# The Fourier branch computed on folded tokens: 129 of 256 output positions, the rest mirrored

## The chip, the cores and the metric

One core of one Trainium2 chip runs the whole program. The metric is the device time of one execution in microseconds (us), lower is better. The kernel before takes 1244.37 us (median of 3 runs, 1244.19 to 1245.08).

The engines are called by the profile's names: PE is TensorE's matrix multiply, PEld its weight loads, DVE is VectorE, ACT is ScalarE, POOL is GpSimd and SP is SyncE, which issues nearly all transfers. Each engine works through its own instructions in order and waits on the others by semaphores.

## The reference, cut to what matters

Two layers run over 256 latent tokens and 256 context tokens with 1024 channels. Every layer normalises and modulates the tokens, projects them with one combined weight (`h @ w_in`), feeds slices of the projection to four branches (retention, short convolution, Fourier mixing, pooling), merges the branches through sigmoid gates and one output projection, and ends with a SwiGLU feed-forward part. The last layer needs only the latent stream after the retention state of the context is known. The branch that changes is this one:

```python
def fourier_mix(u):                        # u: (1, 256 tokens, 256 channels)
    b, n, _ = u.shape
    z = jnp.fft.fft2(u.astype(jnp.float32).reshape(b, n, FFT_GROUPS, FFT_GROUP_DIM), axes=(1, 3), norm='ortho')
    return jnp.real(z).reshape(b, n, MIX).astype(u.dtype)
```

It is a two-dimensional Fourier transform, over 256 tokens and over 64 channels inside each of four groups, of which the real part is kept: with C and S the cosine and sine sums, the result is Cn(Cd u) - Sn(Sd u).

## The kernel before, in words

The kernel is one long list of `Step`s written out in order. A step names the weight blocks it needs, and a loop at the end of the program takes the steps one after the other: it first calls `Weights.pump`, then the step's own function, then (for a step with `tick`) one round of `tick`.

- `Weights` (L54 to L153) streams the weights. A block is 128 partitions by 1024 or 1280 values. It is loaded by SP (L94), cut into a rounded high part by ACT (L102, `hi`) and a low part by DVE (L112, `lo = raw - hi`). Blocks are cut up to two ahead of the step that is being written (`ahead=2`), in a ring of four.
- A projection `proj` (L660) of one block of 128 output channels takes 8 chunks of the contraction with three matmuls each (`mm3`, L205: hi*hi, lo*hi, hi*lo, all in the reduced fp32 type, one pass each). In layer 0 it streams 512 columns (256 latent and 256 context tokens, NS = 2), in layer 1 it streams 256 (NS = 1).
- Small side work, such as the Fourier branch after its projection, is put in a list `sides` of generators. After each ticking step, `tick` (L213) advances the first two of the list to their next `yield` and puts them at the end. The side work therefore sits in every engine's instruction order between the projections of the following steps.
- `bank` (L174) gives out PSUM banks in rotation: four of kind "a", three of kind "b". `ot` (L628) gives out SBUF tiles from a rotating pool of 5 (layer 0) or 4 (layer 1), which the convolution and pooling branches share; `sm` is a pool of small tiles, among them four "hf" tiles that `modulate` (L451) uses.

In layer 0 the order is: the opening with q, k and v, two gate projections (which start the retention side work `both`), then for each half c of the 256 branch channels the Fourier step and three convolution steps (`conv_cg`, `conv_xv`, `conv_bg`), then two pooling steps, then the big gate steps, which read the branch results `br`. In layer 1 the six convolution steps come first, while the context stream's last norms of layer 0's feed-forward part (`Chain`, L483: `one`, `two`, `three`, then four times `turn`, which transposes on PE and modulates on ACT and DVE) still run as side work. Then come the two Fourier steps, two gate steps, `drain_sides`, which writes out all side work that is left, and the value projection `v_step` (L688, tile `vps`).

In the Fourier branch (`fourier`, L853) the projection lands in PSUM with channels on partitions and tokens along the columns. ACT copies it to SBUF (`u`, L857). `rest` is the side work. Its first stage (L866, tile `fa`) transforms the channels: for each stream and each half of 128 tokens, one plain fp32 matmul with 128 tokens as the stationary operand and the 256 columns of `fcs` (cosine beside sine) as the moving one; ACT copies the result to `pf` (L868). Its second stage (L874, tile `fb`) transforms the tokens: per stream four accumulating fp32 matmuls, each with 128 stationary columns of `pf` and 256 moving columns of `fcn`. The result is cut into `br[2]` by `split` (ACT L202, DVE L203). A plain fp32 matmul shows as two PE instructions in the trace, with a weight load before each.

Of the kernel before, what the change touches and what calls it, by code (L numbers as in the profile page):

```python
# [8 lines left out]
F32 = mybir.dt.float32  # L9
F32R = mybir.dt.float32r  # L10
BF16 = mybir.dt.bfloat16
AF = mybir.ActivationFunctionType
ALU = mybir.AluOpType
# [4 lines left out]
P = 128  # L18
D = 1024
KC = D // P  # L20
SEQ = 256
# [8 lines left out]
LOG2E = 1.4426950408889634  # L30
VROW = 528
PIECE = 33
MOD_ORDER = (0, 2, 1, 3)
Q, K, V, G, BG, CG, XV, FU, PU, GATE = 0, 2, 4, 6, 8, 10, 12, 14, 16, 18
KEEP = 4
# [121 lines left out]
def kernel(ctx: ExitStack, tc: tile.TileContext, a: dict, out: bass.AP):  # L157
    ctx.enter_context(tc.manual_schedule())
    nc = tc.nc

    def pool(name, bufs=1, stack=ctx, **kw):
        return stack.enter_context(tc.tile_pool(name=name, bufs=bufs, reuse_waits="tile", **kw))
# [3 lines left out]
    sm = pool("sm", 4)  # L166
# [7 lines left out]
    def bank(tag, name, shape=None, keep=False):  # L174

        i = banks[tag].pop(0)
        if not keep:
            banks[tag].append(i)
        t = psum.tile([P, 512], F32, tag=f"bank{i}", name=name)
        return t if shape is None else cut(t, shape)  # L180
# [4 lines left out]
    def cut(t, shape):  # L185
        n = 1
        for x in shape:
            n *= x
        t = t[:, :n]
        if len(shape) == 2:  # L190
            t = t.rearrange("p (a b) -> p a b", b=shape[1])
        if len(shape) == 3:
            t = t.rearrange("p (a b c) -> p a b c", b=shape[1], c=shape[2])
        return t

    def load(pl, shape, src, name, eng=None, **kw):
        t = pl.tile(shape, F32, name=name, **kw)
        (eng or nc.sync).dma_start(t, src)
        return t

    def split(hi, lo, src):
        nc.scalar.activation(hi, src, AF.Copy)  # L202
        nc.vector.tensor_tensor(lo, src, hi.bitcast(F32), op=ALU.subtract)  # L203

    def mm3(ps, st, mv, first, last):  # L205

        nc.tensor.matmul(ps, lhsT=st[0], rhs=mv[0], start=first, stop=False)  # L207
        nc.tensor.matmul(ps, lhsT=st[0], rhs=mv[1], start=False, stop=False)  # L208
        nc.tensor.matmul(ps, lhsT=st[1], rhs=mv[0], start=False, stop=last)  # L209
# [21 lines left out]
    nc.vector.memset(mhalf, -0.5)  # L231
    two = dec.tile([P, 2 * PIECE], F32, name="two")
    nc.vector.memset(two, 2.0)
# [11 lines left out]
    bsel = load(cst, [P, 2], a["c_bsel"], "bsel", nc.scalar)  # L245
    e12 = load(dec, [P, 2, 2 * PIECE], a["c_e12"], "e12", nc.scalar)
    kexp = load(dec, [P, 2, 2], a["c_kexp"], "kexp", nc.scalar)
# [126 lines left out]
    def decays():  # L374
# [21 lines left out]
        yield  # L396
        y = dec.tile([P, 2 * PIECE], F32, name="dy")
        nc.vector.tensor_scalar(y, e12[:, 0, :], lg[:, 0:1], None, op0=ALU.mult)
        nc.vector.scalar_tensor_tensor(y, e12[:, 1, :], lg[:, 1:2], y, op0=ALU.mult, op1=ALU.add)
        ky = dec.tile([P, DEPTH, 2, 2, HEADS], F32, name="dky")  # L400
        for l in range(DEPTH):
            for jt in range(2):
                for d in range(2):
# [3 lines left out]
                    )  # L407
        v = dec.tile([P, 2 * PIECE], F32, name="dv")
        kf = ky.rearrange("p a b c d -> p (a b c d)")
# [4 lines left out]
        for i in range(2):  # L414
            nc.sync.dma_start(
                vscr[i].rearrange("a (b c) -> (a b) c", c=PIECE), v[:, i * PIECE : (i + 1) * PIECE]
            )
# [195 lines left out]
    def mixer(l, h, hnext, start=None):  # L613
        T = 512 if l == 0 else 256
        NS = T // SEQ
# [6 lines left out]
        def rt(tag, shape, name, bufs=1):  # L622
            n = 1
            for x in shape:
                n *= x
            return cut(P_["t"].tile([P, n], F32, tag=tag, name=name, bufs=bufs), shape)

        def ot(shape, name):  # L628
            return cut(P_["o"].tile([P, T + 32], F32, tag="o", name=name), shape)

        br, fix = [], {}
# [17 lines left out]
        def fixed():  # L649
            t = P_["t"]  # L650
            fix["rope"] = load(t, [P, 2, SEQ], a["c_rope"], f"rope{l}")
            fix["fcs"] = load(t, [P, 2 * P], a["c_fd"], f"fcs{l}")
            fix["fcn"] = load(t, [P, 2, 2, SEQ], a["c_fn"], f"fcn{l}")
            fix["inv"] = load(t, [P, 2, SEQ], a["c_inv"], f"inv{l}")
            for c in range(2):
                for j in range(2):
                    b = slice(j * DH, (j + 1) * DH)
                    nc.sync.dma_start(fix["pw"][b, c, b], a["pool_w"][l, 2 * c + j])

        def proj(blk, name, ps=None, cols=slice(0, T)):  # L660
            if ps is None:
                ps = bank(ptag[0], name)[:, :T]
            for k in range(KC):
                sl = slice(k * P, (k + 1) * P)
                mm3(
                    ps[:, cols],
                    (blk.hi[:, sl], blk.lo[:, sl]),
                    (h[0][k][:, cols], h[1][k][:, cols]),
                    k == 0,
                    k == KC - 1,  # L670
                )
            return ps
# [179 lines left out]

        def fourier(blk, c):  # L853

            ps = proj(blk, f"fu{l}{c}")
            u = ot([T], "fu")
            nc.scalar.activation(u, ps, AF.Copy)  # L857

            def rest():
                yield  # L860
                pf = []
                for s in range(NS):
                    pa = bank("a", f"fa{l}{c}{s}", [2, 2 * P])
                    for t in range(2):
                        lo = s * SEQ + t * P
                        nc.tensor.matmul(pa[:, t, :], lhsT=u[:, lo : lo + P], rhs=fix["fcs"], start=True, stop=True)  # L866
                    pf.append(ot([2, 2 * P], "pf") if NS == 2 else rt("pf", [2, 2 * P], "pf"))
                    nc.scalar.activation(pf[s], pa, AF.Copy)  # L868
                yield
                for s in range(NS):  # L870
                    pb = bank("a", f"fb{l}{c}{s}")[:, :SEQ]
                    for n in range(4):
                        t, j = n // 2, n % 2
                        nc.tensor.matmul(  # L874
                            pb,
                            lhsT=pf[s][:, t, j * P : (j + 1) * P],
                            rhs=fix["fcn"][:, t, j, :],
                            start=(n == 0),
                            stop=(n == 3),
                        )  # L880
                    sl = slice(s * SEQ, (s + 1) * SEQ)
                    split(br[2][0][c][:, sl], br[2][1][c][:, sl], pb)

            sides.append(rest())

# [150 lines left out]
        if l == 0:  # L1036
# [43 lines left out]
            for c in range(2):  # L1080
                add(fourier, FU + c, c)
                conv_steps(c)
# [358 lines left out]
    start = next(i for i, st in enumerate(mix0) if st.tick)  # L1441
# [34 lines left out]
def _layouts(v):  # L1476
# [4 lines left out]
    d["c_in"] = c(np.stack([v["c"][0].reshape(KC, P).T, v["c_ctx"].reshape(KC, P).T], 1))  # L1481
    wm = v["w_mod"][0].reshape(KC, P, 12, 512)[:, :, list(MOD_ORDER)]
    d["w_mod"] = c(wm.reshape(KC, P, 2, 2, 512).transpose(0, 2, 1, 3, 4)).reshape(KC, 2, P, 1024)
# [29 lines left out]
def _constants():  # L1513
    import numpy as np

    f4 = np.float32
    d = {"c_ident": np.eye(P, dtype=f4)}
    p = np.arange(P)
    d["c_bsel"] = ((p[:, None] // DH == np.arange(2)) / DH).astype(f4)
    e = (p[:, None] % 16) * PIECE + np.arange(PIECE) - 256  # L1520
    e = np.concatenate([e, -e], 1)
    d["c_e12"] = np.stack([np.maximum(e, 0), np.maximum(-e, 0)], 1).astype(f4)
    j = p[:, None] + P * np.arange(2)
    d["c_kexp"] = np.stack([255 - j, j], 2).astype(f4)
    freqs = (f4(10000.0) ** (-np.arange(16, dtype=f4) / f4(16))).astype(f4)
    n = np.arange(SEQ)
    pos = np.stack([n // 64, n % 64]).astype(f4)
    ang = pos[(p // 32) % 2] * freqs[p % 16][:, None]
    cos, sin = np.cos(ang).astype(f4), np.sin(ang).astype(f4)
    sin = np.where((p % 32 < 16)[:, None], -sin, sin)  # L1530
    d["c_rope"] = np.stack([cos, sin], 1).astype(f4)
    k = np.arange(DH)
    ph = 2 * np.pi * ((k[:, None] * k) % DH) / DH
    fd = np.zeros((P, 2, P))
    for g in range(2):
        s = slice(g * DH, (g + 1) * DH)
        fd[s, 0, s], fd[s, 1, s] = np.cos(ph), np.sin(ph)
    d["c_fd"] = fd.reshape(P, 2 * P).astype(f4)
    ph = 2 * np.pi * ((n[:, None] * n) % SEQ) / SEQ
    fn = np.stack([np.cos(ph), -np.sin(ph)], 1) / 128.0  # L1540
    d["c_fn"] = np.ascontiguousarray(fn.reshape(2, P, 2, SEQ).transpose(1, 0, 2, 3)).astype(f4)
    inv = np.zeros((P, 2, SEQ))
    for g, w in enumerate((2, 4, 8, 16)):
        cnt = np.clip(n - w // 2 + w, 0, SEQ) - np.clip(n - w // 2, 0, SEQ)
        inv[(g % 2) * DH : (g % 2 + 1) * DH, g // 2] = 1.0 / cnt
    d["c_inv"] = inv.astype(f4)
    return d
# [18 lines left out]
```

## Time and profile before

| | us |
|---|---|
| median of three runs | 1244.37 |
| the profiled execution | 1246.01 |
| its span, first to last instruction | 1244.2 |
| PE busy | 1205.8 |
| PEld busy | 1032.6 |
| DVE busy | 776.5 |
| ACT busy | 452.4 |

The span is what the profile draws; the 1.8 us between it and the execution's own time lie before and after the recorded instructions. Matmuls are pipelined, so the recorded lengths of neighbouring matmuls overlap: what one of them costs in a row of many is the distance from one start to the next, not its recorded length. The mean granted TensorE clock of the execution is 0.994 of full speed (2.4 GHz).

### The profile page before, as it was taken

The page shows a single profiled execution, that of the slowest core. Times are in us where ns is not written, and L with a number is a line of the kernel's source. Part 1 is how long each engine was busy: PE and PEld are TensorE (multiplying, and loading weights), DVE is VectorE, ACT ScalarE, POOL GpSimd, SP SyncE. Part 2 cuts the span into 40 slices and gives each one's busy share as a digit, 9 for nine tenths or more (in the row PEclk, how much of TensorE's full clock was granted, in tenths as well). Part 3 has the DMA queues.
Part 4 walks back from the last instruction along what each step waited for, and adds up shares of the span by engine and source line. Part 5 has one row for each costly group of instructions (what it writes and reads, how often), then busy time and mean ns, then how long its engine had stood idle before and what let it go on. Part 6 is the DMA issues. An engine that isn't in the chain of part 4 may idle for free.

```text
span 1244.2 us, 17237 instructions
## 1 busy us (share of the span) xinstructions
PE 1205.8 (97%) x6790; PEld 1032.6 (83%) x6790; DVE 776.5 (62%) x1242; ACT 452.4 (36%) x712; POOL 41.2 (3%) x39
## 2 busy tenths in 40 slices
PE   6999999999999989999999999989999999999997
PEld 2687878888888788888888888779889998999986
DVE  4454464477887465776777674475666666666644
ACT  3332332323322453222222222354335445444532
POOL 1500000000000000000000000000000000000000
PEclk9999999999999989999999999999999999999999
DMA  8542323546755224666756783343455563656662
GB/s 291 180 130 84 102 85 107 209 151 168 203 176 190 82 94 126 225 209 158 246 185 205 226 270 105 112 134 136 123 153 183 178 225 116 201 176 185 196 220 88
DMA packets 66433, 206.29 MB, mean 166 GB/s; under 512 B 14640, under 2 KB 18224, under 8 KB 66352
## 3 DMA queue, kind: packets, MB, share of 16 engines
q1 hardware_dynamic: 65200, 204.96, 52.8%
q8 instruction: 53, 0.87, 0.3%
q10 hardware_dynamic: 1152, 0.24, 0.1%
q14 instruction: 28, 0.23, 0.1%
HBM read 204.06 MB, written 1.11 MB: 165 GB/s over the span
## 4 chain that ended last, share of the span: by engine, by line
PE 89%; DVE 4%; ACT 3%; issue 1%; DMA 1%; POOL 0%; SPq 0%; DVEq 0%; POOLq 0%; ACTq 0%
PE up L208 10%; PE up L209 10%; PE up L207 10%; PE gate L207 7%; PE gate L209 7%; PE gate L208 7%; PE dn L209 4%; PE dn L208 4%; PE dn L207 4%; PE pb L209 2%; PE pb L207 2%; PE pb L208 2%; PE wo L209 1%; PE wo L207 1%; PE wo L208 1%
## 5 line engine op out<-in xcount | busy, mean ns | idle before, releaser
L317 DVE SCALAR_TENSOR_TENSOR mjunk<-raw_mod,crow 128x1024 bf16<-128x1024 f32 x128 | 156.4, 1222 | 11.1 <-DMA raw_mod<-in_w_modt 8.9
L208 PE MATMUL up<-hm0lo,hi_up 128*128 128x512 f32 (+1 forms) x384 | 143.6, 374 | 0.5 <-DVE hm0lo L449 0.5
L207 PE MATMUL up<-hm0hi,hi_up 128*128 128x512 f32 (+1 forms) x384 | 143.8, 375 | 0.0
L209 PE MATMUL up<-hm0hi,lo_up 128*128 128x512 f32 (+1 forms) x384 | 143.7, 374 | 0.0
L112 DVE TENSOR_TENSOR lo_up<-raw_up,hi_up 128x1024 fp32r<-128x1024 f32 x88 | 107.5, 1223 | 36.2 <-ACT hi_up L102 36.2
L112 DVE TENSOR_TENSOR lo_gt<-raw_gt,hi_gt 128x1280 fp32r<-128x1280 f32 x64 | 95.3, 1489 | 30.5 <-ACT hi_gt L102 30.2
L207 PE MATMUL gate<-h0hi,hi_gt 128*128 128x512 f32 x256 | 100.5, 392 | 0.0
L207 PE MATMUL up<-hm1hi,hi_up 128*128 128x256 f32 x352 | 100.3, 285 | 0.0
L208 PE MATMUL up<-hm1lo,hi_up 128*128 128x256 f32 x352 | 100.3, 285 | 0.0
L209 PE MATMUL up<-hm1hi,lo_up 128*128 128x256 f32 x352 | 100.1, 284 | 0.0
L209 PE MATMUL gate<-h0hi,lo_gt 128*128 128x512 f32 x256 | 99.6, 389 | 0.0
L208 PE MATMUL gate<-h0lo,hi_gt 128*128 128x512 f32 x256 | 99.6, 389 | 0.0
L102 ACT ACTIVATE hi_up<-raw_up 128x1024 fp32r<-128x1024 f32 x88 | 92.1, 1048 | 7.2 <-DMA raw_up<-in_w_up 6.6
L102 ACT ACTIVATE hi_gt<-raw_gt 128x1280 fp32r<-128x1280 f32 x64 | 81.0, 1266 | 28.0 <-DMA raw_gt<-in_w_gate 28.0
L112 DVE TENSOR_TENSOR lo_dn<-raw_dn,hi_dn 128x1024 fp32r<-128x1024 f32 x44 | 53.6, 1224 | 51.4 <-ACT hi_dn L102 51.2
L988 ACT ACTIVATE sg<-gate 128x512 f32<-128x512 f32 (+1 forms) x64 | 31.3, 490 | 148.1 <-PE gate L209 146.8
L208 PEld LDWEIGHTS up<-hm0lo,hi_up 128*128 128x128 f32 x384 | 73.4, 191 | 13.1 <-DVE hm0lo L449 0.7
L207 PEld LDWEIGHTS up<-hm0hi,hi_up 128*128 128x128 f32 x384 | 73.5, 191 | 12.6
L209 PEld LDWEIGHTS up<-hm0hi,lo_up 128*128 128x128 f32 x384 | 73.3, 191 | 12.4
L102 ACT ACTIVATE hi_dn<-raw_dn 128x1024 fp32r<-128x1024 f32 x44 | 46.4, 1058 | 91.8 <-PE dn L209 67.1
L207 PE MATMUL gate<-hf0hi,hi_gt 128*128 128x256 f32 x256 | 73.4, 287 | 0.0
L209 PE MATMUL gate<-hf0hi,lo_gt 128*128 128x256 f32 x256 | 72.4, 283 | 0.0
(327 smaller groups left out, 2759.7 us busy)
## 6 DMA issues: line engine op xcount, KB each, us to landing
raw_up<-in_w_up SPq DMA_DIRECT2D x88, 512.0 KB, 3.9
raw_gt<-in_w_gate SPq DMA_DIRECT2D x64, 640.0 KB, 4.0
raw_mod<-in_w_modt SPq DMA_DIRECT2D x80, 512.0 KB, 4.1
raw_dn<-in_w_down SPq DMA_DIRECT2D x44, 512.0 KB, 4.3
raw_in<-in_w_in SPq DMA_DIRECT2D x28, 512.0 KB, 3.7
raw_mod<-in_w_mod SPq DMA_DIRECT2D x16, 512.0 KB, 4.5
raw_wo<-in_w_o SPq DMA_DIRECT2D x16, 512.0 KB, 4.2
grow<-gscr SPq DMA_DIRECT2D x6, 512.0 KB, 7.4
```

The lines of the kernel that those rows point to most:

```text
L102: self.nc.scalar.activation(b.hi, b.raw, AF.Copy)
L112: self.nc.vector.tensor_tensor(b.lo, b.raw, b.hi.bitcast(F32), op=ALU.subtract)
L207: nc.tensor.matmul(ps, lhsT=st[0], rhs=mv[0], start=first, stop=False)
L208: nc.tensor.matmul(ps, lhsT=st[0], rhs=mv[1], start=False, stop=False)
L209: nc.tensor.matmul(ps, lhsT=st[1], rhs=mv[0], start=False, stop=last)
L317: nc.vector.scalar_tensor_tensor(junk, b.raw, 1.0, crow[s], op0=ALU.mult, op1=ALU.mult, accum_out=out()[:, s, i : i + 1])
L988: nc.scalar.activation(sg, ps, AF.Sigmoid)
```

## The change

With 256 tokens, cos and sin of token n and of token 256-n are equal and opposite, so the sums need only the folded tokens u[n] + u[256-n] (with cosines) and u[n] - u[256-n] (with sines), 128 of each; token 128 stands alone, and its part of output k is (-1)^k times its channel cosine sum. Output 256-k differs from output k only by the sign of the sine part, so 129 outputs are computed and 127 are mirrored.

- `u` gets a zero column behind the 256 tokens of each stream (a DVE memset). Behind the ACT copy, two DVE operations make the folded tiles (`fold`, the second operand read backwards), and a small copy keeps token 128 (`mid`). They stand in the Fourier step itself, not in the side work.
- The first stage has two matmuls per stream, each with 128 moving columns, in place of two with 256. The results of both streams share one bank and one ACT copy.
- The second stage has two matmuls per stream with 129 moving columns, not accumulated, in place of four with 256; and per half c one more with NS columns, the channel cosine sum of `mid`.
- Then, per stream: ACT copies the sine part (and the `mid` column) to SBUF (`si`, from the pool of "hf" tiles), DVE adds the alternating `mid` part to the cosine part, subtracts the sine part into the mirrored columns, and adds it into the plain ones. `split` now stands behind one more `yield`, once for both streams, and reads SBUF.
- `fcn` is 128 x 3 x 129 values in place of 128 x 2 x 2 x 256.

```diff
-            fix["fcn"] = load(t, [P, 2, 2, SEQ], a["c_fn"], f"fcn{l}")
+            fix["fcn"] = load(t, [P, 3, NK], a["c_fn"], f"fcn{l}")
...
             ps = proj(blk, f"fu{l}{c}")
-            u = ot([T], "fu")
-            nc.scalar.activation(u, ps, AF.Copy)
+            u = ot([NS, SEQ + 8], "fu")
+            nc.vector.memset(u[:, :, SEQ : SEQ + 1], 0.0)
+            nc.scalar.activation(u[:, :, :SEQ], ps.rearrange("p (s n) -> p s n", n=SEQ), AF.Copy)
+            eo = ot([2 * T // 2 + NS], "eo")
+            fold = [eo[:, j * NS * P : (j + 1) * NS * P].rearrange("p (s n) -> p s n", n=P) for j in range(2)]
+            mid = eo[:, 2 * NS * P : 2 * NS * P + NS]
+            for j, op in ((0, ALU.add), (1, ALU.subtract)):
+                nc.vector.tensor_tensor(fold[j], u[:, :, :P], u[:, :, P + 1 : SEQ + 1][:, :, ::-1], op=op)
+            nc.vector.tensor_copy(mid, u[:, :, P])
 
             def rest():
                 yield
-                pf = []
+                pa = bank("a", f"fa{l}{c}", [NS, 2, P])
                 for s in range(NS):
-                    pa = bank("a", f"fa{l}{c}{s}", [2, 2 * P])
-                    for t in range(2):
-                        lo = s * SEQ + t * P
-                        nc.tensor.matmul(pa[:, t, :], lhsT=u[:, lo : lo + P], rhs=fix["fcs"], start=True, stop=True)
-                    pf.append(ot([2, 2 * P], "pf") if NS == 2 else rt("pf", [2, 2 * P], "pf"))
-                    nc.scalar.activation(pf[s], pa, AF.Copy)
+                    for j in range(2):
+                        rhs = fix["fcs"][:, j * P : (j + 1) * P]
+                        nc.tensor.matmul(pa[:, s, j, :], lhsT=fold[j][:, s, :], rhs=rhs, start=True, stop=True)
+                pf = ot([NS, 2, P], "pf")
+                nc.scalar.activation(pf, pa, AF.Copy)
                 yield
+                f = ot([NS, SEQ], "ff")
+                part = []
                 for s in range(NS):
-                    pb = bank("a", f"fb{l}{c}{s}")[:, :SEQ]
-                    for n in range(4):
-                        t, j = n // 2, n % 2
+                    pb = bank("a", f"fb{l}{c}{s}")
+                    for j in range(2):
                         nc.tensor.matmul(
-                            pb,
-                            lhsT=pf[s][:, t, j * P : (j + 1) * P],
-                            rhs=fix["fcn"][:, t, j, :],
-                            start=(n == 0),
-                            stop=(n == 3),
+                            pb[:, j * NK : (j + 1) * NK],
+                            lhsT=pf[:, s, j, :],
+                            rhs=fix["fcn"][:, j, :],
+                            start=True,
+                            stop=True,
                         )
-                    sl = slice(s * SEQ, (s + 1) * SEQ)
-                    split(br[2][0][c][:, sl], br[2][1][c][:, sl], pb)
+                    n = NK
+                    if s == 0:
+                        nc.tensor.matmul(pb[:, 2 * NK : 2 * NK + NS], lhsT=fix["fcs"][:, :P], rhs=mid, start=True, stop=True)
+                        n += NS
+                    si = sm.tile([P, SEQ], F32, tag="hf", name=f"fs{s}", bufs=4)
+                    nc.scalar.activation(si[:, :n], pb[:, NK : NK + n], AF.Copy)
+                    part.append(si)
+                    at128 = part[0][:, NK + s : NK + s + 1]
+                    nc.vector.scalar_tensor_tensor(
+                        f[:, s, :NK], fix["fcn"][:, 2, :], at128, pb[:, :NK], op0=ALU.mult, op1=ALU.add
+                    )
+                    nc.vector.tensor_tensor(
+                        f[:, s, NK:][:, ::-1], f[:, s, 1 : NK - 1], si[:, 1 : NK - 1], op=ALU.subtract
+                    )
+                    nc.vector.tensor_tensor(f[:, s, :NK], f[:, s, :NK], si[:, :NK], op=ALU.add)
+                yield
+                split(br[2][0][c], br[2][1][c], f.rearrange("p s n -> p (s n)"))
```

## Rows read from the trace of the kernel before

**Rows 1.** The page: span, busy time, share of the span and instructions of each engine.

```profile
span 1244.2 us, 17237 instructions
PE 1205.8 (97%) x6790; PEld 1032.6 (83%) x6790; DVE 776.5 (62%) x1242; ACT 452.4 (36%) x712; POOL 41.2 (3%) x39
```

**Rows 2.** The page: the chain that ended last, share of the span by engine.

```profile
PE 89%; DVE 4%; ACT 3%; issue 1%; DMA 1%; POOL 0%; SPq 0%; DVEq 0%; POOLq 0%; ACTq 0%
```

**Rows 3.** Waits of PE: line, what it waited for, us in total, times, longest.

```profile
PE xt L531 <- DVE prod L522: 10.6, 6, 2.6
...
PE fb L874 <- ACT pf L868: 0.3, 1, 0.3
```

**Rows 4.** Groups of PE instructions by line and shape: busy us, mean ns of one.

```profile
L874 PE MATMUL fb<-fcn,pf 128*128 128x256 f32 x48 | 11.2, 383 | 0.3 <-ACT pf L868 0.3
...
L866 PE MATMUL fa<-fcs,fu 128*128 128x256 f32 x24 | 5.9, 384 | 0.0
```

**Rows 5.** Order of time on PE, layer 0, first half: start, us, line, operation, count.

```profile
102.58 1.99 PE L866 MATMUL fa<-fcs,fu 128*128 128x256 f32 x8
104.22 0.58 PE L207 MATMUL xv<-h0hi,hi_in 128*128 128x512 f32 x1
...
111.05 3.72 PE L874 MATMUL fb<-fcn,pf 128*128 128x256 f32 x16
114.42 0.58 PE L207 MATMUL bg<-h0hi,hi_in 128*128 128x512 f32 x1
```

**Rows 6.** Order of time on PE, layer 0, the retention's small matmuls.

```profile
127.77 0.95 PE L821 MATMUL var<-bsel,ys 128*128 128x2 f32 x8
128.57 0.49 PE L207 MATMUL cg<-h0hi,hi_in 128*128 128x512 f32 x1
...
134.16 0.60 PE L835 MATMUL yr<-ident,rx 128*128 128x128 f32 x4
134.60 1.89 PE L866 MATMUL fa<-fcs,fu 128*128 128x256 f32 x8
```

**Rows 7.** Order of time on PE, layer 1, from the second gate step to the value projection.

```profile
851.02 1.89 PE L874 MATMUL fb<-fcn,pf 128*128 128x256 f32 x8
852.75 1.03 PE L866 MATMUL fa<-fcs,fu 128*128 128x256 f32 x4
...
854.47 1.99 PE L874 MATMUL fb<-fcn,pf 128*128 128x256 f32 x8 [0.25 <-ACT pf L868]
856.11 0.47 PE L207 MATMUL vps<-hi_v,hf0hi 128*128 128x256 f32 x1
856.41 0.28 PE L208 MATMUL vps<-lo_v,hf0hi 128*128 128x256 f32 x1
856.53 0.28 PE L209 MATMUL vps<-hi_v,hf0lo 128*128 128x256 f32 x1
```

**Rows 8.** Groups of DVE instructions by line and shape.

```profile
L764 DVE TENSOR_TENSOR vd<-v,kdec 128x128 f32<-128x128 f32 x16 | 3.6, 283 | 0.0
...
L203 DVE TENSOR_TENSOR br<-fb,br 128x256 fp32r<-128x256 f32 x6 | 2.4, 419 | 2.6 <-ACT br L202 2.6
```

**Rows 9.** Groups of ACT instructions by line and shape.

```profile
L868 ACT ACTIVATE pf<-fa 128x512 f32<-128x512 f32 x6 | 3.4, 590 | 1.4 <-PE fa L866 1.4
...
L783 ACT ACTIVATE st<-st 128x128 f32<-128x128 f32 x4 | 1.1, 273 | 0.4 <-PE st L775 0.4
```

**Rows 10.** Order of time on ACT, layer 0: the copy of the Fourier projection.

```profile
94.94 0.60 ACT L857 ACTIVATE fu<-fu 128x512 f32<-128x512 f32 x1 [4.47 <-PE fu L209]
```

**Rows 11.** Order of time on DVE, layer 1: weight cuts around the Fourier and gate steps.

```profile
842.76 1.49 DVE L112 TENSOR_TENSOR lo_gt<-raw_gt,hi_gt 128x1280 fp32r<-128x1280 f32 x1 [1.95 <-ACT hi_gt L102]
...
846.93 1.22 DVE L112 TENSOR_TENSOR lo_v<-raw_v,hi_v 128x1024 fp32r<-128x1024 f32 x1 [1.55 <-ACT hi_v L102]
```

**Rows 12.** Order of time on ACT, layer 1: before the second half's copy.

```profile
849.61 1.04 ACT L102 ACTIVATE hi_v<-raw_v 128x1024 fp32r<-128x1024 f32 x1
850.56 0.36 ACT L988 ACTIVATE sg<-gate 128x256 f32<-128x256 f32 x1
```

More of the change, by code (lines that the diff above doesn't have):

```diff
@@ L32 @@
 PIECE = 33
+NK = SEQ // 2 + 1
 MOD_ORDER = (0, 2, 1, 3)
@@ L1539, in _constants @@
     ph = 2 * np.pi * ((n[:, None] * n) % SEQ) / SEQ
-    fn = np.stack([np.cos(ph), -np.sin(ph)], 1) / 128.0
-    d["c_fn"] = np.ascontiguousarray(fn.reshape(2, P, 2, SEQ).transpose(1, 0, 2, 3)).astype(f4)
+    ph = ph[:P, :NK]
+    fn = np.stack([np.cos(ph), -np.sin(ph), np.broadcast_to((-1.0) ** np.arange(NK), (P, NK))], 1) / 128.0
+    d["c_fn"] = np.ascontiguousarray(fn).astype(f4)
     inv = np.zeros((P, 2, SEQ))
```

## The prediction

> **What bounds the kernel now.** I read the page's busy times first, then the chain, then the waits of PE, then the order of time around the Fourier work. PE is busy 1205.8 of 1244.2 us [rows 1], and the chain of work that ended last lies on PE for 89% of the span [rows 2], so time taken off PE comes off the end unless another engine is late there. The longest sum of waits of PE is for the normalised rows at the ends of the layers' parts, 10.6 us [rows 3]; that chain of DVE and ACT work starts when a part's last matmul is done, whenever that is, and it keeps its length. PE waits for the Fourier work itself only once, 0.3 us in the second half of layer 1 [rows 3]. So the branch is PE work that runs back to back with the projections around it, and the stage to look at is its own stretch in each layer.
>
> **PE: what goes.** The branch has 24 PE instructions in the first stage and 48 in the second [rows 4], two for each of 12 and 24 fp32 matmuls. Their recorded lengths overlap, so I take distances between starts. First stage, layer 0: 8 instructions from 102.58 to the next group's start at 104.22, 1.64 us, 0.205 each [rows 5]. Second stage: 16 in 3.37 us, 0.211 each [rows 5]; in layer 1, 8 in 1.73 us and 8 in 1.64 us, 0.216 and 0.205 [rows 7]. With 0.205 for the first and 0.21 for the second stage, 24 x 0.205 + 48 x 0.21 = 4.9 + 10.1 = 15.0 us of PE time go.
>
> **PE: what comes.** Per half c, layer 0 has four first-stage and four second-stage matmuls of 128 or 129 columns, layer 1 two and two. Over both halves that is 24 matmuls, 48 PE instructions, and four more matmuls (8 instructions) of one or two columns for token 128. The trace of before has no plain fp32 matmul with full 128 x 128 stationary part and 128 columns, so I bound it. From below: four transposes, which stream 128 fp32 columns, start 0.44/4 = 0.11 us apart [rows 6]. The nearest row in occupation is the projection of layer 1: a one-pass matmul of 256 columns behind a 128 x 128 weight load, 0.12 us from start to start [rows 7]; an instruction of a plain fp32 matmul took 0.21 us for 256 columns, so at 128 it should occupy PE for about 0.105 us, as the one-pass one does. From above: a load alone. Eight instructions with two columns each took 0.80 us, 0.10 each [rows 6], though there is hardly anything to stream; if that load were not hidden behind the stream before it, an instruction would cost 0.10 + 0.105 = 0.205 us. I take 0.12, since that row has the same load and the same occupation. The very small ones I take at 0.10 from the two-column row, below it only if their loads hide better. So 48 x 0.12 + 8 x 0.10 = 5.8 + 0.8 = 6.6 us come, and PE is relieved of 15.0 - 6.6 = 8.4 us: about 5.7 us in layer 0 and 2.7 us in layer 1. The 129th column is worth 1/128 of 0.105 us, nothing here.
>
> The Trainium skill speaks against this step: "TensorE: Matmul & The Clock Gate", section "Part 3: Packing small matmuls" says that a weight load overlaps a running matmul only where the two use different row groups. By it every instruction here, all rows in use, would pay load and stream one after the other. The projections of layer 1 disagree: their loads and streams use all 128 rows, and 0.12 us from start to start is less than a 0.10 us load plus 0.105 us of stream [rows 6, 7]. I keep the rule as the second rival, with its price made of those rows.
>
> **DVE and ACT in layer 0.** Per half c the change adds two folds of 256 columns (0.419 each by the 256-column row), a memset and a small copy (at most 0.283 each, the length at 128 columns), and per stream three operations of 127 to 129 columns (0.283 each) [rows 8]: 0.84 + 0.57 + 6 x 0.283 = 3.1 us at most, 6.2 us over both halves. ACT loses one copy of 0.590 and gains two of some 0.273 [rows 9], so nothing. What hides it: the copy of the projection runs at 94.94 to 95.54 [rows 10], the folds can be done by about 96.6, and PE asks for them only at 102.58 [rows 5], behind a whole projection. Queued behind the waiting folds on DVE are the retention's mask product, needed by PE at the same tick, and a low part of a weight block that is two steps from its use; both have over 3 us in hand. In the second half the variance step of the retention is queued behind the folds, and the transposes that wait for it start at 134.16 [rows 6], over 5 us behind its matmuls at 127.77. The reading back of the result stands behind the convolution's work, and its `br` is read many projections later. I take 0 for all of it; without that cover it is the 6.2 us and the waits of DVE for ACT's copies, which the third rival prices. Backward reading I take as free (below it there is nothing to gain).
>
> **DVE and ACT in layer 1.** Here the engines are tighter. ACT and DVE pass work in a ring around each step: weight low part, modulated row, its high part, next weight's high part, next low part. Two successive low parts start at 842.76 and 846.93, 4.2 us apart [rows 11], while PE needs some 3.6 us for a gate step, 30 matmuls at 0.12 us [rows 7]. The fold of 128-token tiles adds 2 x 0.283 plus the two small operations, some 0.7 us, to this ring in each of the two Fourier steps. The low part of a gate block is cut two steps ahead, so it has about 3 us in hand and stays hidden. What is late is the copy `pf` of the second half. Before, ACT was through with the sigmoid at 850.9 [rows 12] and waited for PE. Now the sigmoid ends near 850.9 + 1.4 - 0.2 (a `pf` of half the width) = 852.1, then come the new `si` copy (0.27) and `pf` (some 0.4, between the two rows of [rows 9]), so the second stage can start at about 852.9. PE gets there at 854.47 - 0.25 [rows 7] less what it has saved by then: 4 x (0.205 - 0.12) = 0.34 us in each first stage and 1.73 - 0.68 = 1.05 in the first half's second stage, so at about 852.5. The wait becomes 0.4 us by this, and up to 1 us if the sigmoid is a little later, where it was 0.25. I charge 0.5 us; the ends are -0.3 (the wait goes) and 3.6 us: two halves with 2 x 0.283 + 2 x 0.283 + 3 x 0.283 of DVE time, 4.0 us, less the 0.4 us that ACT's narrower `pf` copies give back, all on the path.
>
> **Loads and tiles.** `fcn` shrinks from 524 to 198 KB. Inside the Fourier stretches PE waits for nothing but `pf` [rows 3], so 0, with perhaps 0.3 us to gain. The rotating pool gets four tiles per half in both layers where it got three or one; each tile that is taken over had its last reader at least one projection earlier, so I charge nothing.
>
> **Sum.** -8.4 + 0.5 = -7.9 us. Against the profiled execution's own 1246.0 us that is 1238.1; the profiled execution lies 1.6 us over the median, and the runs to compare with are those, so 1244.4 - 7.9 = 1236.5 us.
>
> **Rivals.**
> 1. The ring of layer 1 takes more: with the whole 3.6 us on the path the time is 1244.4 - 8.4 + 3.6 = 1239.6. For it: that stretch is tight, and DVE's queue is strict. Against it: only one wait of 0.25 us is there now, and the weights are cut ahead. 15%.
> 2. Loads don't hide behind 128 columns: 48 x 0.205 + 0.8 = 10.6 us come instead of 6.6, so 1236.5 + 4.0 = 1240.5. For it: a load's own pace (0.10) is as long as the new stream, so there is no margin. Against it: the projections' 0.12 us. 8%.
> 3. Slower: DVE's queue becomes the path in both layers. Its head waits for ACT's copy of the projection, and everything behind it, weight cuts first, starts late, so that PE waits for a low part. The price is the added DVE work, 6.2 + 4.0 us, plus the waits for ACT's copies in front of it, 2 x (0.6 + 2 x 0.27) in layer 0 and 2 x (0.4 + 0.27) in layer 1, 3.6 us: 13.8 us against 8.4 saved, 1249.8. It decides from 8.4 us on PE. For it: the folds stand in the step itself and not in the side work. Against it: DVE is busy 62% of the span, and low parts are cut two steps ahead. 3%.
>
> **How the numbers follow.** My forecast has 72%, the rivals 15, 8 and 3%, and 2% is for what I don't see. Its own lower end is a record pitch of 0.11 (another 0.5 us), no wait (0.5 + 0.3) and the smaller load (0.3): 1234.9; I set 1234.5. The range reaches over both mild rivals to 1240.6. A difference under 0.2% (2.5 us) cannot be told from none here; all but the third rival and part of the unseen are faster by more. Faster 92%, same 4%, slower 4%.
>
> **What would show it.** In the new trace: 24 `fa` and 32 `fb` instructions (24 of 129 columns, 8 tiny) with starts 0.11 to 0.12 us apart; a wait of `fb` for `pf` in layer 1 of under 1 us; no wait of PE for folds; the granted clock unchanged. Starts 0.2 us apart would show the second rival, waits of the value or gate projections for a low part in the fold's wake the first or third. The forecast fails if PE's total wait grows by over 2 us or PE's busy time falls by much less than 8 us.

## The result and the profile after

The changed kernel takes 1235.38 us (median of 4 runs, 1234.56 to 1235.83) against 1244.72 us of the kernel before beside it (4 runs, 1244.19 to 1245.12): a ratio of 0.9924, interval 0.9908 to 0.994, or 9.3 us less. The forecast was 1236.5.

The page of the changed kernel, with the lines that answer to [rows 1, 2]:

```profile
span 1232.8 us, 17240 instructions
PE 1196.1 (97%) x6774; PEld 1025.4 (83%) x6774; DVE 783.7 (64%) x1274; ACT 452.1 (37%) x714; POOL 41.1 (3%) x39
```

```profile
PE 89%; DVE 4%; ACT 3%; issue 1%; DMA 1%; POOL 0%; SPq 0%; DVEq 0%; POOLq 0%; ACTq 0%
```

PE's busy time fell by 9.7 us, DVE's rose by 7.2, ACT's stayed, and the chain that ended last still lies on PE for 89%. The two profiled spans differ by 11.4 us, 2 more than the medians; the section after the experiments says which part of that is not the change's.

The longest wait of PE in the changed kernel (line, what it waited for, us in total, times, longest):

```profile
PE xt L532 <- DVE prod L523: 10.7, 6, 2.6
```

The long wait of [rows 3] is unchanged. The one of `fb` for `pf`, to which the forecast added 0.5 us, has left the list (0.04 us of it remain in the trace). No line of the list names a fold.

Order of time on PE, layer 0, first half, and then layer 1 from the first Fourier step to the value projection (start, us, line, operation, count; lines are one higher than before ahead of the Fourier function):

```profile
101.64 1.16 PE L875 MATMUL fa<-fcs,eo 128*128 128x128 f32 x8
102.55 0.47 PE L208 MATMUL xv<-h0hi,hi_in 128*128 128x512 f32 x1
102.87 0.39 PE L209 MATMUL xv<-h0lo,hi_in 128*128 128x512 f32 x1
...
109.28 0.71 PE L884 MATMUL fb<-fcn,pf 128*128 128x129 f32 x4
109.83 0.28 PE L893 MATMUL fb<-eo,fcs 128*128 128x2 f32 x2
109.97 0.69 PE L884 MATMUL fb<-fcn,pf 128*128 128x129 f32 x4
110.42 0.48 PE L208 MATMUL bg<-h0hi,hi_in 128*128 128x512 f32 x1
...
835.73 0.61 PE L875 MATMUL fa<-fcs,eo 128*128 128x128 f32 x4
836.10 0.36 PE L208 MATMUL gate<-hf0hi,hi_gt 128*128 128x256 f32 x1
...
843.79 0.61 PE L884 MATMUL fb<-fcn,pf 128*128 128x129 f32 x4
844.24 0.28 PE L893 MATMUL fb<-eo,fcs 128*128 128x1 f32 x2
844.38 0.69 PE L875 MATMUL fa<-fcs,eo 128*128 128x128 f32 x4
844.90 0.60 PE L532 MATMUL xt<-ident,prod 128*128 128x128 f32 x4
845.54 0.71 PE L884 MATMUL fb<-fcn,pf 128*128 128x129 f32 x4
846.09 0.28 PE L893 MATMUL fb<-eo,fcs 128*128 128x1 f32 x2
846.23 0.36 PE L208 MATMUL vps<-hi_v,hf0hi 128*128 128x256 f32 x1
846.43 0.28 PE L209 MATMUL vps<-lo_v,hf0hi 128*128 128x256 f32 x1
```

Read as in [rows 5, 7], from a group's start to the next group's: in the first half of layer 0 the first stage went from 1.64 to 0.91 us, the second from 3.37 to 1.14. In layer 1 the last second stage took 1.64 and now 0.69, with no wait ahead of it.

By line and shape the page of groups has 24 `fa` and 32 `fb` instructions, eight of them tiny, where [rows 4] have 24 and 48.

### The profile page after: what moved, and what is told of

The parts are those of the page before. It is cut to its first block, busy times and chain, and to the rows that moved or that the text cites. A ratio compares the mean times of both kernels' runs of the same rounds, so it can differ in the third digit from the quotient of the medians.

```text
span 1232.8 us, 17240 instructions
## 1 busy us (share of the span) xinstructions
PE 1196.1 (97%) x6774; PEld 1025.4 (83%) x6774; DVE 783.7 (64%) x1274; ACT 452.1 (37%) x714; POOL 41.1 (3%) x39
## 4 chain that ended last, share of the span: by engine, by line
PE 89%; DVE 4%; ACT 3%; issue 1%; DMA 1%; POOL 0%; SPq 0%; DVEq 0%; POOLq 0%; ACTq 0%
PE up L210 10%; PE up L209 10%; PE up L208 10%; PE gate L208 7%; PE gate L210 7%; PE gate L209 7%; PE dn L210 4%; PE dn L209 4%; PE dn L208 4%; PE pb L208 2%; PE pb L210 2%; PE pb L209 2%; PE wo L210 1%; PE wo L208 1%; PE wo L209 1%
```

## The experiments

Diffs are against the changed kernel where nothing else is said. The ratios are to the kernel before, run beside each experiment (medians 1244.34, 1244.68 and 1244.15 us in the three sets).

**1. The PE work alone.** The changed matmuls and their `pf` copies, with the rest of the ACT and DVE work as before.

```diff
-            (memset, two folds, copy of token 128)
-                        nc.tensor.matmul(pa[:, s, j, :], lhsT=fold[j][:, s, :], ...
+                        nc.tensor.matmul(pa[:, s, j, :], lhsT=u[:, s, j * P : (j + 1) * P], ...
-                    (si, three DVE operations per stream, one split of f)
+                    split(br[2][0][c][:, sl], br[2][1][c][:, sl], pb[:, :SEQ])
```

> The matmuls of the changed kernel with the ACT and DVE work of the kernel before: the folds, the small copy and the reading back are left out (the first stage reads the unfolded tokens, split reads PSUM as before), so the values are not those of the reference. Theory (all of the gain is PE stream time, the added ACT and DVE work is hidden): the same time as the changed kernel, 1235.4 within 0.7, 9.3 us under the kernel before. Rival (the added DVE work costs something in layer 1's tight stretch): 1 to 3.6 us faster than the changed kernel, 1231.8 to 1234.4.

Measured 1234.36 us, ratio 0.992 (0.9903 to 0.9936). The changed kernel has 0.9924, and 0.9921 (0.9906 to 0.9936) when it was run again in the second set (1234.52 us). The number lies at the upper edge of the rival's range, but the changed kernel moved down with it: the ACT and DVE work costs 0.1 to 0.5 us by the ratios, with more than 2 us of uncertainty. So the times alone don't rule the rival out at its lower end; the profiles say more, and the section on the prediction reads them.

**2. The ACT and DVE work alone**, with the matmuls of before (diff against the kernel before).

```diff
+            (memset, two folds, copy of token 128: as changed)
-                    split(br[2][0][c][:, sl], br[2][1][c][:, sl], pb)
+                    (si, three DVE operations per stream: as changed)
+                split(br[2][0][c], br[2][1][c], f.rearrange("p s n -> p (s n)"))
```

> The matmuls of the kernel before with the ACT and DVE work of the changed kernel added: folds are made and not used, the reading back works on the wide result, so the Fourier branch's values are not the reference's. Theory (hidden): 1244.7 within 0.7, as the kernel before. Rival (the DVE queue or layer 1's ring is on the path): 1 to 4 us slower, up to 1248.7.

Measured 1244.57 us, ratio 1.0005 (0.9995 to 1.0014): nothing, and at most 1.7 us. A wait of PE in its profile, the same as in [rows 3]:

```profile
PE fb L884 <- ACT pf L876: 0.3, 1, 0.3
```

So 6.6 us more of DVE work (783.1 against 776.5 us busy) left PE's one wait where it was. The theory (hidden) held. Two things this run cannot show: no matmul reads the folds here, so PE never asks for them, and PE takes its old time, so the other engines have more room than in the changed kernel.

**3. Wide.** As many matmuls as in the changed kernel, each with 255 or 256 columns.

```diff
-                        rhs = fcs[:, j * P : (j + 1) * P]
+                        rhs = fcs            # 256 columns, half of them read
-                            rhs=fix["fcn"][:, j, :],
+                            rhs=(255 columns of fix["fcn"])
```

> The changed kernel with 256 moving columns in the first stage and 255 in the second, of which 128 and 129 are used; the number of matmuls stays. Theory (an instruction costs its columns): 48 instructions go from 0.108 to 0.21 us, +4.9 us, and what is left of the last one of a group before the next group starts doubles, 7 times 0.1, so 1241.0 within 0.8. Rival (the number of instructions, by their weight loads, sets the time, not the columns): no more than 1 us over the changed kernel.

Measured 1241.05 us, ratio 0.997 (0.996 to 0.998). Order of time on PE, layer 0, first half:

```profile
101.38 1.99 PE L875 MATMUL fa<-fcs,eo 128*128 128x256 f32 x8
103.02 0.58 PE L208 MATMUL xv<-h0hi,hi_in 128*128 128x512 f32 x1
...
109.85 1.13 PE L884 MATMUL fb<-fcn,pf 128*128 128x255 f32 x4
...
111.71 0.58 PE L208 MATMUL bg<-h0hi,hi_in 128*128 128x512 f32 x1
```

The first stage is back at 1.64 us, its length before [rows 5]; the second stage, with half as many large matmuls as before, takes 1.86. All eight groups add up to 10.5 us, against 14.7 before and 6.1 in the changed kernel. By the ratios the halved number of second-stage matmuls is worth 3.7 us and the halved width some 6.

**4. Narrow.** The same matmuls with 64 and 65 columns.

```diff
-                        rhs = fcs[:, j * P : (j + 1) * P]
+                        rhs = fcs[:, j * P : j * P + P // 2]
-                            rhs=fix["fcn"][:, j, :],
+                            rhs=fix["fcn"][:, j, :65],
```

> The changed kernel with 64 moving columns in the first and 65 in the second stage; half of the transform is left out. Theory (a weight load of 0.10 us is the floor under an instruction): 48 x 0.008 + 7 x 0.05, 0.7 us under the changed kernel at most, 1234.7 to 1235.4, and starts 0.10 us apart. Rival (the stream alone sets the distance): starts 0.055 us apart, 48 x 0.054 + 0.35 = 2.9 us less, 1232.5.

Measured 1233.94 us, ratio 0.9917 (0.9903 to 0.9932). Order of time on PE, as above:

```profile
100.76 1.10 PE L875 MATMUL fa<-fcs,eo 128*128 128x64 f32 x8
101.67 0.48 PE L208 MATMUL xv<-h0hi,hi_in 128*128 128x512 f32 x1
...
108.39 0.66 PE L886 MATMUL fb<-fcn,pf 128*128 128x65 f32 x4
...
109.53 0.48 PE L208 MATMUL bg<-h0hi,hi_in 128*128 128x512 f32 x1
```

The stages take 0.91 and 1.14 us, to the hundredth what they take with twice the columns; over all eight groups it is 6.01 against 6.07 us. So at 128 columns a matmul instruction already goes at the pace of something that does not depend on the columns. The weight loads show what. Order of time on PEld, the first stage of the changed kernel and then of this one:

```profile
101.64 0.97 PEld L875 LDWEIGHTS fa<-fcs,eo 128*128 128x128 f32 x8 [0.38 <-ACT cgs L958]
102.53 0.19 PEld L208 LDWEIGHTS xv<-h0hi,hi_in 128*128 128x128 f32 x1
```

```profile
100.75 0.97 PEld L875 LDWEIGHTS fa<-fcs,eo 128*128 128x128 f32 x8 [0.39 <-ACT cgs L960]
101.64 0.19 PEld L208 LDWEIGHTS xv<-h0hi,hi_in 128*128 128x128 f32 x1
```

In both, a load starts every 0.111 us, eight of them up to the first load of the next group. In the changed kernel the loads of the tiny matmuls keep that distance too (starts at 109.72, 109.83 and 109.94 us). It is not a pace that every PE instruction has: four transposes in the changed kernel's opening, with a stationary part of 64 x 128 and 64 columns, start their loads 0.06 us apart:

```profile
23.03 0.33 PEld L279 LDWEIGHTS modt<-ident,modrows 64*128 64x128 f32 x4 [1.60 <-ACT modrows L1367]
```

So the loads of a full 128 x 128 stationary part follow one another at 0.111 us, and this is the floor. The rival (half the columns, half the time) is out.

**5 and 6. One layer alone.** The change in layer 0 only, then in layer 1 only; the other layer has the Fourier function and the `fcn` of before.

```diff
+        fourier = fourier_new if l in (0,) else fourier_old     # (1,) in the second
```

> The change in layer 0 only. Theory (PE stream time only): its four groups take 3.90 us in the profile after where they took 9.82 before, and what is left of each last instruction is 0.1 us less, so 6.3 us under the kernel before (within 1). Rival (DVE's queue costs in layer 0): under 5 us.

> The change in layer 1 only. Theory: groups of 2.17 us where there were 4.92, 0.2 us left over and the wait of 0.25 us gone, 3.1 us under the kernel before (within 1). Rival (layer 1's ring of ACT and DVE eats part of it): under 2 us, with a wait of the second stage for pf of 0.5 us or more.

Layer 0: 1237.59 us, ratio 0.9943 (0.9929 to 0.9958), -7.1 us. Layer 1: 1242.04 us, ratio 0.9978 (0.9969 to 0.9988), -2.7 us. Together 9.8 by the ratios, and the whole is 9.5 and 9.8 by its own two: no exchange between the layers that these times could show.

**7. The changed kernel again**, in the set of 5, 6 and 8, so that the parts have the whole beside them.

> The changed kernel itself, beside the parts. Theory and rivals alike: 9.3 us under the kernel before within 1.5. The profile is for the wait of the second stage in layer 1: if the rival of layer 1's ring holds, it is over 0.5 us in a trace whose clock is full there; by the theory it is under 0.3 us.

1234.52 us, ratio 0.9921, as given under 1. In its profile `fb` waits 0.04 us for `pf`, but the clock is at half for two stretches of layer 1 there too, so it does not say what the wait is at full clock.

**8. The DVE work three times.** Folds and the three reading-back operations written out three times each.

```diff
+                for _ in range(3):
                     nc.vector.tensor_tensor(fold[j], ...
...
+                    for _ in range(3):
                         (the three operations on f)
```

> The changed kernel with each fold and each of the three reading-back operations of DVE done three times (the subtraction and addition are repeated, so the branch's values are not the reference's): about 10 us more DVE work in layer 0 and 6 us in layer 1. Theory (there is slack to spare in layer 0, little in layer 1): 0 to 1 us from layer 0 and 1 to 3 us from layer 1, so 1 to 4 us over the changed kernel. Rival (the added DVE work is already at its limit): two thirds of it or more on the path, 10 us or more over it.

Measured 1238.23 us, ratio 0.9947 (0.993 to 0.9964): 3.2 to 3.7 us over the changed kernel, as the theory has it. Waits of PE, layer 1, in the order of time:

```profile
841.34 0.66 PE L532 MATMUL xt<-ident,prod 128*128 128x128 f32 x4 [0.51 <-DVE hf L463]
...
847.77 0.71 PE L885 MATMUL fb<-fcn,pf 128*128 128x129 f32 x4 [0.34 <-ACT pf L878]
```

Here is the mechanism of the first rival: the ring arrives late, and PE waits for a modulated row and for `pf`. In the profile layer 1's stretch from the first convolution projection to the value projection is 1.5 us longer than in the changed kernel's profile, and layer 0's to the first gate 0.7; part of the rest is two more stretches at half clock. In the profiles of the changed kernel neither wait is there, but in layer 1 not much is left in hand.

**9 to 11. Two kernels profiled once more, and one without the matmuls of token 128.** The profiles of the changed kernel had two stretches at half clock in layer 1's Fourier stretch, those of the first experiment and of the kernel before none there.

```diff
-                    if s == 0:
-                        nc.tensor.matmul(pb[:, 2 * NK : 2 * NK + NS], ..., rhs=mid, ...)
-                        n += NS
```

> The changed kernel, unchanged, profiled once more. Open: in its two profiles so far layer 1's Fourier stretch holds two stretches of 3.4 us with the clock granted at half (the first projection starts are 0.21 us apart there and not 0.12), and the profile without the changed ACT and DVE work has none. Theory: they are tied to the kernel's own order of work, so they are there again, near 821 and 832 us from the span's start, and the stretch from the first convolution projection of layer 1 to the value projection is 42.8 us again, within 0.2. Rival: chance of their phase; then this profile has them elsewhere or not at all, and the stretch is 41.3 us.

> The kernel with the changed PE work and the ACT and DVE work of before, profiled once more; its Fourier result is not the reference's. Theory (half-clock stretches tied to the kernel): again none in layer 1's Fourier stretch, 41.3 us from the first convolution projection to the value projection. Rival (chance): one or two there, 42 to 43 us.

> The changed kernel without the matmuls of token 128 (two in each layer, eight PE instructions taken as 4 matmuls of two passes), so that the part of token 128 in the output is wrong. Theory (an instruction costs its weight load's pace or less, 0.07 us from start to start here, and nothing waits for these): 0.6 us less than the changed kernel, 1233.8 to 1235.0, with the stages' starts otherwise unchanged. Rival (the small matmuls break the row and cost a full 0.2 us each, or their result holds up the reading back): 1.5 to 2.5 us less, 1232.0 to 1233.2.

The changed kernel has the two stretches once more, in 42.9 us from `cg` to `vps`, but so has the second profile of the first experiment's kernel, which had none in its first. (The two new executions took 1236.78 and 1233.27 us; 3.1 of the 3.5 us between them lie in the opening, ahead of the first transposes at 25.41 and 22.34 us.) Busy time by stretch for experiment 1's kernel, first profile and then second (window, its length, PE, PEld, DVE, ACT, POOL busy with counts, granted clock, DMA share, GB/s):

```profile
820.00:824.00 4.00, 2.97 (x23) 2.77 (x23) 2.32 (x5) 2.39 (x5) 0.54 (x1) 1.00 0.00 0
...
830.00:835.00 5.00, 4.18 (x36) 4.18 (x37) 2.97 (x5) 3.82 (x8) 0.00 (x0) 1.00 0.32 88
...
1030.00:1040.00 10.00, 8.09 (x60) 6.95 (x60) 7.93 (x16) 5.90 (x15) 1.08 (x2) 0.89 0.33 107
```

```profile
820.00:824.00 4.00, 4.00 (x24) 3.98 (x22) 2.33 (x7) 2.39 (x5) 0.54 (x1) 0.57 0.00 0
...
830.00:835.00 5.00, 5.00 (x32) 5.00 (x31) 3.05 (x4) 2.84 (x6) 0.00 (x0) 0.66 0.55 186
...
1030.00:1040.00 10.00, 8.01 (x67) 6.83 (x65) 7.88 (x16) 6.16 (x16) 1.08 (x2) 1.00 0.31 103
```

The same program, once with full clock in the first two windows and a dip in the third, once the other way round. From `cg` to `vps` it took 41.35 us (803.66 to 845.01) and 42.85 us (802.44 to 845.29). So a kernel does not have them in every execution; the theory that I had put down for them fell. They are not spread evenly over the kernels either: of the nine profiles with the shortened matmuls in layer 1 (three of the changed kernel, two of experiment 1, and 4, 6, 8 and 11) eight have both, of the four with 256 columns there (the kernel before, 2, 3 and 5) none. In seven of those eight the dip in the feed-forward part is missing. Whether the shorter matmuls make the two stretches likelier, and what in an execution decides, is open.

Without the matmuls of token 128 the median is 1235.52 us (ratio 0.9929, 0.9911 to 0.9947), no gain, against 0.6 expected; its four runs spread over 2.7 us, so the time decides nothing here. The trace does. Order of time on PE, layer 1:

```profile
843.12 0.61 PE L884 MATMUL fb<-fcn,pf 128*128 128x129 f32 x4
843.56 0.61 PE L875 MATMUL fa<-fcs,eo 128*128 128x128 f32 x4
...
844.64 0.71 PE L884 MATMUL fb<-fcn,pf 128*128 128x129 f32 x4
845.11 0.36 PE L208 MATMUL vps<-hi_v,hf0hi 128*128 128x256 f32 x1
```

The second stages take 0.44 and 0.47 us where they took 0.59 and 0.69. Over all eight groups it is 5.18 against 6.07 us: 0.89 us for the eight instructions, 0.11 each. The rival's 0.2 us for each is out, and so is the theory's 0.07: an instruction with one or two columns costs as much as one with 128, since each has a full weight load. The distances inside a group (0.28 us recorded, 0.14 from start to start for two) make them look cheaper than they are.

## Why the prediction was right, step by step

**PE: what goes.** Forecast 15.0 us; the eight groups of before, start to next group's start, add up to 14.74. Right within 0.3.

**PE: what comes.** Forecast 6.6 us, measured 6.07 in the changed kernel's eight groups, so PE is relieved of 8.7 us where the forecast had 8.4. By the profile without the tiny matmuls, the 48 large ones take 5.18 us, 0.108 each, against 0.12 taken, and the eight tiny ones 0.11 each, against 0.10. The row that the step chose, the projection of layer 1, was the right neighbour, but for a reason that the step gave only half: at 128 columns a stream is as short as the load, and experiment 4 shows the loads' pace, 0.111 us, to be what is left. The second rival (loads not hidden, 0.205) is out by the first stage's 0.91 us for 8. The rule behind it, in the Trainium skill, "TensorE: Matmul & The Clock Gate", section "Part 3: Packing small matmuls", does not hold here: loads with all rows in use overlapped streams with all rows in use, or eight of both would not fit into 0.91 us. The same page's section "LDWEIGHTS (loading the stationary operand)" prices a load by its columns alone at columns / 1.2 in ns, which makes an estimate of 107 ns for 128. The 0.111 us from load to load agrees with that; the opening's loads of 64 rows and 128 columns, 0.06 us apart, follow one another faster than it would give.

**What the sum left out.** The first instruction behind a group is recorded as starting when the group's last one has hardly begun, so what is left of the last one shows in the distance after it. Before, 0.42 us lay between the first two `xv` matmuls behind the first stage (104.22 and 104.64) and 0.30 between the first two `vps` [rows 7]; after, 0.32 (102.55, 102.87) and 0.20 (846.23, 846.43). The shorter last instruction gives back 0.1 us at six such places, 0.6 us. The step that took a group's end to be the next group's first start missed it.

**DVE and ACT in layer 0, charged at nothing.** Right: experiment 2 shows no time, experiment 8 only 0.7 us for three times the work. The profiles settle it: from the first Fourier projection to the first gate the changed kernel takes 70.19 us in each of its three profiles, and experiment 1, without the folds and the reading back, 70.18 in both of its own. From the opening's end to the first gate the profile is 6.4 us shorter, of which the PE groups are 5.9 and the four remainders 0.4.

**DVE and ACT in layer 1, charged at 0.5.** This term was mis-sized for what the profiles show: `fb` waits 0.04 us for `pf`, where it waited 0.25, and not 0.75. The ring did lengthen as worked out. Order of time on DVE and then on ACT in the changed kernel:

```profile
830.55 1.49 DVE L113 TENSOR_TENSOR lo_gt<-raw_gt,hi_gt 128x1280 fp32r<-128x1280 f32 x1
...
832.17 0.49 DVE L866 TENSOR_TENSOR eo<-fu 128x128 f32<-128x128 f32 x2
...
835.13 1.49 DVE L113 TENSOR_TENSOR lo_gt<-raw_gt,hi_gt 128x1280 fp32r<-128x1280 f32 x1 [1.95 <-ACT hi_gt L103]
...
839.77 1.23 DVE L113 TENSOR_TENSOR lo_v<-raw_v,hi_v 128x1024 fp32r<-128x1024 f32 x1 [1.34 <-ACT hi_v L103]
```

```profile
843.40 0.36 ACT L1013 ACTIVATE sg<-gate 128x256 f32<-128x256 f32 x1
844.55 0.28 ACT L896 ACTIVATE fs<-fb 128x130 f32<-128x130 f32 x1 [0.79 <-PE fb L893]
845.11 0.38 ACT L877 ACTIVATE pf<-fa 128x256 f32<-128x256 f32 x1 [0.27 <-PE fa L875]
```

From the first `lo_gt` to the second sigmoid it is 12.85 us, where it was 11.70 (838.86 to 850.56): 1.15 more, and 1.2 was the forecast's figure. Experiment 3, with the same ACT and DVE work and the full clock there, has 12.85 as well. From `lo_gt` to `lo_v` it is 4.64, where [rows 11] have 4.17. But ACT then waits for PE, 0.79 and 0.27 us, and not PE for ACT. Two things made the difference.

The old wait of 0.25 us is gone because the copy `pf` takes 0.38 us and not 0.60; experiment 1, which has the short copy but not the longer ring, shows the same 0.04 us, and experiment 2, with the long copy, still the 0.25.

And the new wait needs PE to be early: the step had it 1.7 us earlier by the saved matmuls. From the transposes at the start of the first Fourier projection to the end of the work before the last second stage, PE took 15.4 us before (838.85 to 854.22), 13.5 in experiment 1's first profile at full clock (830.82 to 844.29), but 15.0 in the changed kernel (830.54 to 845.50), since in every profile of the changed kernel a stretch at half clock lies in that projection. At full clock PE would be there 13.5 us after the first `lo_gt`, and ACT would end `pf` at about 13.7 to 13.9 (the sigmoid from 12.85 on, 0.36, then `fs` and `pf`, 0.28 and 0.38, which overlap a little): a wait of 0.2 to 0.4 us. That is an estimate from these rows; no profile here shows that case. So the longer ring is shown, the wait at full clock is not, and that no cost came up in the profiles is in part luck of where the clock fell.

**The profiled pair.** Of the 11.4 us between the spans, 0.9 lie in the opening, where PE waits for the first weights (its transposes start at 23.98 and 23.04 us; in other executions from 22.12 to 25.41). 6.4 are layer 0's Fourier part, 0.8 come between there and layer 1, mostly from a stretch at half clock that is twice as long in the profile before (granted clock from 440 to 460 us: 0.83 there, 0.91 after), 1.8 are layer 1's stretch with two stretches at half clock that the profile before does not have there, and 1.6 lie behind, where the profile before has such a stretch and the one after none. Layer 1's stretch without them is experiment 1's 41.35 us against 44.6 before (44.4 and 44.5 in experiments 2 and 5), 3.1 to 3.3 us: the groups' 2.75, the 0.2 us of the wait that went and 0.2 of remainders. With both stretches at half clock experiment 1 takes 42.85 us and the changed kernel 42.87 to 42.90, so the ACT and DVE work costs nothing there either. 6.4 + 3.1 to 3.3, some 9.6 us, is what the traces give for the change at full clock; the ratios give 9.5 and 9.8.

So the forecast's -7.9 was short by 0.3 (PE's groups), 0.6 (remainders) and 0.5 to 0.7 (a wait that went instead of growing), within the stated range. The first and third rivals need PE to wait for DVE or ACT behind the fold; it took three times the work to see the first begin. One slip in the chances: the forecast and the two mild rivals are all faster and have 95% between them, where the prediction gives 92% to faster. And of its signs one held only in the mean: the granted clock is 0.994 before and 0.995 after, but the stretches at half clock lie elsewhere.

## What to carry to other kernels

When PE bounds a stretch, count its instructions and their start-to-start pitch, and take the pitch from the row with the same weight load and the same stream time. Halving the columns paid down to the point where the loads set the pace (here 128 columns of plain fp32, 0.111 us); below it, half the columns gave nothing, and an instruction with two columns cost as much as one with 128, so there only fewer instructions help. Work moved to DVE for it was free in layer 0, where its consumer lies a whole projection later, and tripling the added work is a quick way to see how much slack is left.

## What the runs showed of the hardware

- Plain fp32 matmuls with a full 128 x 128 stationary part: 0.205 us per PE instruction at 256 columns, 0.114 at 128 and at 64 (0.91 us for 8 in both), and 0.11 with one or two columns (0.89 us for 8). At 128 columns and below, their weight loads start 0.111 us apart.
- TensorE's granted clock fell from 2.4 to 1.2 GHz (projections 0.21 us apart and not 0.12) for short stretches. In the changed kernel they came in layer 1 behind waits of PE of 1.3 and 0.8 us (for `bg`) and of 2.6 us (for `xt`). The same waits stand in experiment 1's first profile, and the clock stayed full there; so the same program had the stretches at different places. One in the feed-forward part cost 1.2 to 1.3 us (experiment 1's two profiles; experiments 2 and 5), two in layer 1's Fourier stretch together 1.5 (41.35 and 42.85 us); two waits of `fu`, 0.3 and 0.8 us, are gone where the clock is half.
- The added DVE operations, groups by line and shape (busy us, mean ns of one):

```profile
L899 DVE SCALAR_TENSOR_TENSOR ff<-fcn,fs,fb 128x129 f32<-128x129 f32 x6 | 2.1, 345 | 0.0
L905 DVE TENSOR_TENSOR ff<-ff,fs 128x129 f32<-128x129 f32 x6 | 1.8, 295 | 0.2
...
L866 DVE TENSOR_TENSOR eo<-fu 128x128 f32<-128x128 f32 x4 | 1.0, 290 | 0.2
```

The one that reads PSUM (`fb`) and has three operands takes 0.345 us, the one of the same size from SBUF 0.295; which of the two differences makes it was not tried apart. Reading the second operand backwards cost next to nothing: 0.290 us per fold, against 0.283 for a plain operation of that size [rows 8].
